# Fourteen tiny loads behind the weight load of the third last group of a batched matmul

## The chip, the core and the metric

The kernel runs on one core of one Trainium2 chip. The metric is the device time in microseconds. Three runs of the kernel before gave 518.32, 518.4 and 518.6 us, median 518.4.

## The reference

```python
b1, b2, m, k, n = 8, 16, 256, 512, 384
x:      (b1, b2, m, k) float32, weight: (b1, b2, k, n) float32
np.matmul(x, weight).astype(np.float32)
```

So there are 128 independent products of a 256x512 matrix with a 512x384 matrix. Inputs are 64 MiB of x and 96 MiB of weights, the output is 48 MiB.

## The kernel before

The 128 products are taken in NG = 32 groups of G = 4. For a group, x is 1024 rows of 2 KB, laid on 128 partitions with 8 rows each (`x_sb`, 2 MB); the weight is 2048 rows of 1.5 KB, laid on 128 partitions with 16 rows each (`w_sb`, 3 MB); the output is 1024 rows (`out_sb`, 1.5 MB). There are two buffers of `x_sb`, two of `w_sb` and four of `out_sb`.

Each engine runs its own written-out program, and semaphores tie them together:

- SP (`on_sync`) issues all transfers, on one DMA queue. `load_x` (L108) first waits until the casts of the group two earlier have freed the buffer; `load_w` (L125) waits likewise for the casts on VectorE and ScalarE (L119, L120); `store` (L138) waits until the output has been copied out. Per group the order is `load_x(n)`, `store(n - 4)`, `load_w(n)`. The first four groups stand ahead of a loop (groups 4 to 27), the last four behind it (L256 to L260). The first four groups and the last two are "short": their weight load goes out in two halves. Group 31 has no store between its loads. After the loads come the stores of groups 27 to 31, the last in four pieces (L262), and a wait for the completion semaphores of all four output buffers (L264).
- VectorE (`on_vector`) casts x to bf16 (L149, four instructions a group) and 11 of the 16 pieces of the weight (L162, or L178 for short groups).
- TensorE (`on_tensor`) transposes x against an identity (L201) and multiplies (L219).
- ScalarE (`on_scalar`) copies the transposes out of PSUM (L188), casts the other 5 pieces of the weight (L162) and copies the products to `out_sb` (L233).

A completed transfer adds 16 to its semaphore. x, weights and output have their own semaphores for each buffer (`x_in`, `w_in` or `h_in`, `o_out`).

The change touches the declarations at the top (behind L98) and the end of `on_sync` (L256 to L264).

Of the kernel before, what the change touches and what calls it, by code (L numbers as in the profile page):

```python
# [12 lines left out]
def kernel(  # L13
# [14 lines left out]
    x_rows = x.rearrange("b1 b2 m k -> (b1 b2 m) k")  # L28
# [3 lines left out]
    fp32 = mybir.dt.float32  # L32
# [13 lines left out]
    NG = B // G  # L46
# [15 lines left out]
    def sbuf(name, shape, dtype, n):  # L62
        return [
            ctx.enter_context(nc.sbuf_tensor(f"{name}{s}", shape, dtype)) for s in range(n)
        ]
# [6 lines left out]
    def sems(name, n):  # L72
        return [tc.alloc_semaphore(f"{name}{s}") for s in range(n)]
# [22 lines left out]
    )  # L96
    x_in, w_in, o_out = sems("x_in", XS), sems("w_in", WS), sems("o_out", OS)
    h_in = sems("h_in", G)  # L98


    BIAS = 8
# [2 lines left out]
    def load_x(e, t, U, s):  # L104
        n = t * U + s
        if not isinstance(n, int) or n >= XS:
            e.wait_ge(x_cast, n * T + (1 - XS) * T)
        e.dma_start(  # L108
            x_sb[s % XS][:],
            x_rows[bass.ds(n * (G * M), G * M)].rearrange("(p r) k -> p r k", r=R),  # L110
        ).then_inc(x_in[s % XS], 16)

    def is_short(n):
        return isinstance(n, int) and (n < LAG or n >= NG - 2)

    def load_w(e, t, U, s):
        n = t * U + s
        if not isinstance(n, int) or n >= WS:
            e.wait_ge(w_vcast, n * CV + (1 - WS) * CV)  # L119
            e.wait_ge(w_acast, n * CA + (1 - WS) * CA)  # L120
        d = SL // SH if is_short(n) else 1
        k = SL * KO // d
        for h in range(d):
            sem = h_in[s % WS * 2 + h] if is_short(n) else w_in[s % WS]
            e.dma_start(  # L125
                w_sb[s % WS][:, h * k : (h + 1) * k, :],
                w_rows[bass.ds(n * (G * K) + h * (G // d * K), G // d * K)].rearrange(
                    "(p k) n -> p k n", k=k
                ),
            ).then_inc(sem, 16)  # L130

    def store(e, t, U, s, pieces=1):
        n = t * U + s
        dram = o_rows[bass.ds(n * (G * M), G * M)].rearrange("(p r) n -> p r n", r=R)
        for q in range(pieces):
            rows = slice(q * R // pieces, (q + 1) * R // pieces)
            e.wait_ge(o_copied, n * T + ((q + 1) * T // pieces + BIAS))
            e.dma_start(out=dram[:, rows], in_=out_sb[s % OS][:, rows]).then_inc(  # L138
                o_out[s % OS], 16
            )  # L140
# [103 lines left out]
    def on_sync(e):  # L244
        U = OS
        for n in range(LAG):
            load_x(e, 0, NG, n)
            load_w(e, 0, NG, n)
        rounds = (NG - 2 - LAG) // U
        with e.Fori(0, rounds) as t:  # L250
            for s in range(U):
                load_x(e, t, U, LAG + s)
                store(e, t, U, s)
                load_w(e, t, U, LAG + s)

        for n in range(LAG + rounds * U, NG):  # L256
            load_x(e, 0, NG, n)
            if n < NG - 1:
                store(e, 0, NG, n - LAG)
            load_w(e, 0, NG, n)  # L260
        for n in range(NG - 1 - LAG, NG):
            store(e, 0, NG, n, T if n == NG - 1 else 1)  # L262
        for s in range(OS):
            e.wait_ge(o_out[s], 16 + 16 * (NG // OS + (T - 1 if s == (NG - 1) % OS else 0)))  # L264

# [75 lines left out]

    on_gpsimd(nc.gpsimd)
    on_sync(nc.sync)
    on_vector(nc.vector)
    on_tensor(nc.tensor)
# [31 lines left out]
```

## Time and profile before

| | |
|---|---|
| median of three runs | 518.4 us (518.32 to 518.6) |
| span of the profiled execution, first to last instruction | 516.8 us |
| time of the profiled execution beyond its span | not given by the page |
| mean granted TensorE clock | 0.780 |
| ScalarE, VectorE, TensorE busy | 410.3, 397.7, 315.2 us |
| x loads | 32 of 2048 KB, median 22.3 us from issue to landing |
| whole weight loads | 26 of 3072 KB, 18.1 us |
| half weight loads | 12 of 1536 KB, 16.6 us |
| whole stores | 31 of 1536 KB, 25.4 us |
| store pieces | 4 of 384 KB, 5.6 us |
| HBM traffic | 167.77 MB read, 50.33 MB written |

The span is cut by the page into 40 equal slices; a digit there is the busy share of an engine, or of the 16 DMA engines together, in tenths. Times within the span count from its first instruction. A load or store of this kernel leaves 16 completion marks, one for each DMA engine; the trace has the time of each, and of every DMA packet.

### The profile page before, as it was taken

How to read it: one execution, taken by the hardware profiler on the slowest of the kernel's cores; microseconds unless marked ns; L12 is line 12 of the kernel's file. 1: busy time of each engine (PE TensorE's matmuls, PEld its weight loads, DVE VectorE, ACT ScalarE, POOL GpSimd, SP SyncE). 2: the span in 40 equal slices, each digit the busy share in tenths (PEclk: the TensorE clock that was granted, in tenths of full speed). 3: DMA queues.
4: the chain of work that ended last, by engine and by line, in shares of the span. 5: the costliest groups of instructions: out<-in, count | busy, mean ns of one | idle time of the engine just before them, and what ended most of it. 6: DMA issues, size and time to landing. Idle time of an engine off the chain costs nothing.

```text
span 516.8 us, 11572 instructions
## 1 busy us (share of the span) xinstructions
PE 315.2 (61%) x4608; PEld 225.4 (44%) x4608; DVE 397.7 (77%) x462; ACT 410.3 (79%) x387; POOL 0.7 (0%) x6
## 2 busy tenths in 40 slices
PE   2277838555676675765475766558656667565681
PEld 2255525444454443454353544435534445344550
DVE  2788757798777897777987778977779777797960
ACT  1365666998797989798979879978989897899561
POOL 0000000000000000000000000000000000000000
PEclk9687786878786778787778868776867786688887
DMA  8999999999999999999999999999999999999995
GB/s 335 426 428 425 435 429 423 431 430 434 429 424 431 432 439 434 424 426 433 434 434 431 422 432 433 435 429 428 425 438 429 440 428 420 433 433 429 424 428 219
DMA packets 15127, 218.19 MB, mean 422 GB/s; under 512 B 1680, under 2 KB 1680, under 8 KB 2192
## 3 DMA queue, kind: packets, MB, share of 16 engines
q1 hardware_dynamic: 15120, 218.11, 99.0%
q8 instruction: 3, 0.05, 0.0%
q14 instruction: 4, 0.03, 0.0%
HBM read 167.77 MB, written 50.33 MB: 422 GB/s over the span
## 4 chain that ended last, share of the span: by engine, by line
DMA 57%; DVE 29%; issue 9%; PE 1%; SPq 1%; DVEq 1%; ACT 0%
DMA w_sb<-in_weight_dram 57%; DVE w_bf L162 20%; DVE x_bf L149 5%; DVE w_bf L178 4%; PE po L219 1%; SPq L125 0%; DVEq L288 0%; SPq L108 0%; DVEq L158 0%; ACT out_sb L233 0%; SPq L120 0%; DVEq L146 0%; DVEq L172 0%; SPq L372 0%; SPq L60 0%
## 5 line engine op out<-in xcount | busy, mean ns | idle before, releaser
L162 DVE CAST w_bf<-w_sb 32x1536 bf16<-32x1536 f32 x286 | 271.9, 951 | 81.6 <-DMA w_sb<-in_weight_dram 73.5
L219 PE MATMUL po<-w_bf,x_t 128*32 128x384 bf16 x4096 | 200.6, 359 | 38.3 <-DVE w_bf L162 21.0
L201 PE MATMUL pt<-identity,x_bf 128*128 128x128 f32 x512 | 115.0, 415 | 152.2 <-DVE x_bf L149 152.2
L162 ACT CAST w_bf<-w_sb 32x1536 bf16<-32x1536 f32 x130 | 190.9, 1468 | 6.0 <-DMA w_sb<-in_weight_dram 2.8
L201 PEld LDWEIGHTS pt<-identity,x_bf 128*128 128x128 f32 x512 | 103.4, 224 | 164.1 <-issue 163.8
L219 PEld LDWEIGHTS po<-w_bf,x_t 128*32 128x32 bf16 x4096 | 122.0, 106 | 115.9 <-issue 40.7
L233 ACT COPY out_sb<-po 128x768 f32<-128x768 f32 x128 | 101.5, 803 | 57.3 <-PE po L219 56.6
L188 ACT COPY x_t<-pt 128x1024 bf16<-128x1024 bf16 x128 | 120.3, 1025 | 22.1 <-PE pt L201 21.5
L149 DVE CAST x_bf<-x_sb 128x1024 bf16<-128x1024 f32 x128 | 80.0, 688 | 12.4 <-DMA x_sb<-in_x_dram 11.5
L178 DVE CAST w_bf<-w_sb 64x1536 bf16<-64x1536 f32 x48 | 45.9, 955 | 8.3 <-DMA w_sb<-in_weight_dram 7.0
L188 ACT ACT_TABLE_LOAD x1 | 1.3, 1283 | 10.8 <-PE pt L201 10.8
masks.py:199 POOL TENSOR_SCALAR_AFFINE_SELECT identity<-identity 128x128 f32<-128x128 f32 x1 | 0.3, 294 | 0.2 <-POOL identity L239 0.2
L239 POOL MEMSET identity<- 128x128 f32 x1 | 0.2, 205 | 0.5 <-SPq L60 0.5
L361 POOL MEMSET const-bfloat16-1.0<- 128x1 bf16 x1 | 0.1, 102 | 0.0
L361 POOL MEMSET const-uint8-127<- 128x1 uint8 x1 | 0.1, 102 | 0.0
L361 POOL MEMSET const-float32-0.0<- 128x1 f32 x1 | 0.1, 99 | 0.2 <-issue 0.2
L361 POOL MEMSET const-float32-1.0<- 128x1 f32 x1 | 0.1, 99 | 0.0
## 6 DMA issues: line engine op xcount, KB each, us to landing
w_sb<-in_weight_dram SPq DMA_DIRECT2D x26, 3072.0 KB, 18.1
x_sb<-in_x_dram SPq DMA_DIRECT2D x32, 2048.0 KB, 22.3
out_dram<-out_sb SPq DMA_DIRECT2D x31, 1536.0 KB, 25.4
w_sb<-in_weight_dram SPq DMA_DIRECT2D x12, 1536.0 KB, 16.6
out_dram<-out_sb SPq DMA_DIRECT2D x4, 384.0 KB, 5.6
```

The costliest lines, as they stand in the source:

```text
L149: e.tensor_copy(out=x_bf[s % BS][:, rows].rearrange("p r (s q c) -> p r s q c", s=S, c=KO), in_=x_sb[s % XS][:, rows].rearrange("p r (q s ...
L162: copy(out=w_bf[(s * G + i) % WBS][h * C : (h + 1) * C], in_=w_sb[s % WS][i * C : (i + 1) * C, h * KO : (h + 1) * KO, :],).then_inc(w_vcas ...
L178: e.tensor_copy(out=w_bf[(n * G + d * SH + a) % WBS][h * p : (h + 1) * p], in_=w_sb[n % WS][a * p : (a + 1) * p, r : r + KO, :],).then_inc ...
L188: e.copy(out=x_t[s % TS][:, 2 * q : 2 * q + 2], in_=pt[(s * T + q) % PT][:].bitcast(bf16),).then_inc(t_copied, 1)
L201: ins = e.transpose(pt[(s * T + q) % PT][:, rr, h, :], words[:, 2 * q + rr, h :: KO // 2], identity[:],)
L219: ins = e.matmul(po[(s * T + q) % PO][mine, rr, :N], x_t[s % TS][:, 2 * q + rr, ko // 2, mine, ko % 2], w_bf[(s * G + i) % WBS][:, ko, :], ...
L233: e.copy(out=out_sb[s % OS][:, 2 * q : 2 * q + 2, :], in_=po[(s * T + q) % PO][:, :, :N],).then_inc(o_copied, 1)
L239: e.memset(identity[:], 0.0).then_inc(id_done, 1)
L361: nc = _bacc.Bacc("TRN2", target_bir_lowering=False, num_devices=1)
```

## The change

Sixteen small buffers of 16 rows of 64 bytes and sixteen semaphores are declared. When the loads of group 29 (NG - 3) have been issued, fourteen loads follow: for k from 2 to 15, k rows of 64 bytes each, from the first 16 columns of the rows 16k and on of x, into the first k partitions of a buffer of their own, each with its own semaphore. They wait for nothing, and nothing of the computation reads these buffers. At the end, SP waits for the fourteen semaphores too.

```diff
     h_in = sems("h_in", G)
+    probe = sbuf("probe", [16, 16], fp32, 16)
+    few_in = sems("few_in", 16)
...
             load_w(e, 0, NG, n)
+            if n == NG - 3:
+                for k in range(2, 16):
+                    e.dma_start(probe[k][:k], x_rows[16 * k : 17 * k, :16]).then_inc(few_in[k], 16)
         for n in range(NG - 1 - LAG, NG):
             store(e, 0, NG, n, T if n == NG - 1 else 1)
+        for k in range(2, 16):
+            e.wait_ge(few_in[k], 16)
         for s in range(OS):
```

In the built program the fourteen loads stand on SP directly behind the weight load of group 29 and ahead of the wait for the x buffer of group 30. No other engine's order is changed.

## Prediction

> **What bounds the kernel now.** I read the page's share by queue first, then its forty slices, then the chain of waits, SP's timeline from 449 us, and last the windows of the final six microseconds.
>
> ```profile
> span 516.8 us, 11572 instructions
> ...
> DMA  8999999999999999999999999999999999999995
> ...
> q1 hardware_dynamic: 15120, 218.11, 99.0%
> ```
>
> SP's one queue keeps the 16 DMA engines busy for 99.0% of the span, from the second slice to the last but one. No compute engine is above 79%. The page's chain names DVE casts and weight loads in turn, but that chain cannot be shortened below the bytes: one group is 2 MB of x, 3 MB of weight and 1.5 MB of output. The windows of one group each (416.7 to 432.6, 449.2 to 465.1 and 465.1 to 481.0) last 15.90 us at 429 to 432 GB/s with a DMA share of 1.00 to 1.01. So DMA bounds the kernel up to its last stores. Now SP near the end:
>
> ```profile
> 432.58 0.34 SPq L125 DMA_DIRECT2D w_sb<-in_weight_dram  x1
> 432.97 0.42 SPq L108 DMA_DIRECT2D x_sb<-in_x_dram  x1
> 433.44 0.43 SPq L138 DMA_DIRECT2D out_dram<-out_sb  x1
> 449.25 0.33 SPq L125 DMA_DIRECT2D w_sb<-in_weight_dram  x1
> 449.62 0.43 SPq L108 DMA_DIRECT2D x_sb<-in_x_dram  x1
> 450.10 0.44 SPq L138 DMA_DIRECT2D out_dram<-out_sb  x1
> 465.13 0.81 SPq L125 DMA_DIRECT2D w_sb<-in_weight_dram  x2
> 465.99 0.44 SPq L108 DMA_DIRECT2D x_sb<-in_x_dram  x1
> 481.03 0.81 SPq L125 DMA_DIRECT2D w_sb<-in_weight_dram  x2
> ```
>
> Columns are start and duration. SP issues for 1.3 us a group and then stands at a weight wait (L120, L125) for some 14 us. Group 29's weights go out at 449.25, and the tiny loads will stand directly behind them. The chain of waits, in order of time, has this load landing 18.36 us later, the last one 11.08:
>
> ```profile
> 449.25 18.36 DMA w_sb<-in_weight_dram
> ...
> 481.03 11.08 DMA w_sb<-in_weight_dram
> ```
>
> The sixteen completion marks of each load in the trace tell more. Those of x(29), issued at 432.97, fall at 452.58 to 456.58; of store(25), issued next, at 456.23 to 460.31; of w(29) at 463.51 to 467.61; of x(30) at 468.40 to 472.46. Thus the queue is served in order, it is over 14 us deep at 449.6, and the slowest DMA engine is 4 us behind the first. That spread is 3.2 us at 416, 3.9 at 437, 4.1 at 476 and 5.4 at 506. It sets the end:
>
> ```profile
> 509.00:510.00 1.00, 0.00 (x0) 0.00 (x0) 0.00 (x0) 0.00 (x0) 0.00 (x0) 1.00 0.92 372
> 510.00:511.00 1.00, 0.00 (x0) 0.00 (x0) 0.00 (x0) 0.00 (x0) 0.00 (x0) 1.00 0.45 181
> 511.00:512.00 1.00, 0.00 (x0) 0.00 (x0) 0.00 (x0) 0.00 (x0) 0.00 (x0) 0.55 0.22 89
> 512.00:513.00 1.00, 0.00 (x0) 0.00 (x0) 0.00 (x0) 0.00 (x0) 0.00 (x0) 0.50 0.06 25
> 513.00:514.00 1.00, 0.00 (x0) 0.00 (x0) 0.00 (x0) 0.00 (x0) 0.00 (x0) 0.50 0.07 28
> 514.00:515.00 1.00, 0.00 (x0) 0.00 (x0) 0.00 (x0) 0.00 (x0) 0.00 (x0) 0.50 0.05 22
> ```
>
> The last two columns are DMA share and GB/s. A share of 0.06 is one engine in sixteen: from 512.1 to 514.9 one laggard works alone. The last store piece lands at 515.31 and SP's final wait (L264) ends at 515.3; 1.5 us of closing instructions follow. The piece was issued at 506.60, while the first engine finished its share only at 510.41. So compute is not late here: the last matmuls could slip some 2.8 us (510.41 less 506.60 less about 1 us, the time from the first issue at 0.96 to the first packet at 1.98) before any engine missed them.
>
> **The change, part by part.**
>
> *SP's issues.* Fourteen issues are put ahead of x(30) at 449.62; they wait for nothing. A tiny issue is not in the trace. The nearest rows are back-to-back issues of 128 rows, 0.43 us plus 0.05 between, 0.48 together; the longest, in the opening microseconds, took 0.66, so 0.71. The lower end is one 0.05 us gap each. That makes 0.7 to 9.9 us; I take 14 x 0.48 = 6.7 us, since the instruction is of the same form. Behind it on SP stand x(30), store(26) and the wait for w(30). x(30) then goes out at 456.3, store(26) at 456.8, and SP is at its weight wait by 457.3, where it stands until 465.13 anyway: w(30) is not moved. In the queue, x(30) is needed when w(29) is done, 463.51 on the first engine; less 1.0 us from issue to first packet, that is 462.5. Cover is 12.9 us, or 0.92 us a load. Cost: **nothing**, and bandwidth is not lost even at 9.9.
>
> *The rows themselves.* 2 + ... + 15 = 119 rows of 64 bytes, 7.6 KB in all, and a completion mark on each engine used. Spread over 430 GB/s, the bytes are 0.02 us. What counts is the row as a packet: a mark of 4 bytes took 0.009 us in the packet records, a 3072-byte row of the last stores 0.121 us. One row and one mark cost an engine between 0.018 and 0.13 us; by size the row is far nearer to the mark, and I take 0.02 with its mark. No engine can have fewer than 0 or more than 14 of either (one row per load), so the laggard pays 0 to 1.8 us; with half of them, 7 x 0.02 = **0.14 us**. The other engines pay too, but have 3 us and more to spare against the laggard.
>
> The Trainium skill ("DMA: Bandwidth & Descriptors", Why a DMA increments its semaphore by 16 and not by 1) says that such a load uses as many engines as divide both row counts, the lowest-numbered ones, and that the issuing sequencer writes the missing part of the 16 itself. By that rule engines 0 and 1 get 14 rows, engine 14 one, engine 15 none, and the sum would be 0 to 0.28 us instead of 0.14; no run here shows it yet.
>
> *The waits at the end.* The built program's order on SP puts fourteen more semaphores into the final wait; two of them stand behind that of the last store. The loads themselves land by about 470 at the latest, so each wait is met. An SP wait of this kind takes 17 to 28 ns, 0.05 to 0.08 us from start to start; the ones ahead run during the last store's flight (506.9 to 515.3). Two are on the path: **+0.1 us**, bounds 0 and 0.4 (should all of them come after).
>
> *Sum.* 516.8 + 0 + 0.14 + 0.1 = 517.0 us of span, bounds 516.8 and 519.0. The page gives no time of the profiled execution beyond its span; the three runs shown (518.32, 518.4, 518.6) have their median 1.6 us above it. I carry that over: **518.6 us**, +0.05%, where 0.2% (1.04 us) is about what a measurement of this kernel can tell from no change. "Same" thus reaches from 517.4 to 519.4.
>
> **Rivals.**
>
> *Each tiny load exposes a latency (slower).* At the start, when the queue was empty, 16 KB packets took 1.04 to 1.94 us instead of the usual 0.61: 0.43 to 1.33 us of exposed start-up. If an engine could not run on past a tiny row before it has come, it would pay this per load: 14 x 0.43 = 6.0 us, at most 14 x 1.33 = 18.6. On the laggard all of it shows; on the second-latest engine (done at 512.1) what exceeds 3.1 us; on the earliest what exceeds 4.9. It decides from 0.22 us a load (3.1/14). Result: 518.4 + 6.0 - 4.9 = 519.5 at the least, 537 at the most; by the second-latest engine at 0.43, 521.3, and 524.4 on the laggard. Against it: over a group the packets of x (8 x 0.612 + 0.009), w (8 x 0.912 + 0.009) and store (8 x 0.46 + 0.009) add up to 15.9 us, exactly the group's length, so marks and the reads behind them hide completely. But those reads are 12 to 24 KB, and 14 tiny ones in a row have no such length to hide in. The skill's same page (Rules for kernel authors) advises coalescing small transfers, as under 64 KB one pays mostly overhead; its fixed cost of about 2.0 us for a DMA (Anatomy of one DMA, told of GpSimd's path) would make 28 us if nothing overlapped. The trace speaks against that: the four 384 KB stores end 1.0 us apart. Chance 0.22.
>
> *The queue runs dry (slower).* If a tiny issue took over 0.92 us, x(30) would come late for the first engine; the laggard, which has w(29) until 467.61, is hit from (466.6 - 449.6)/14 = 1.21 us. At 1.4 us: 14 x 0.19 = 2.7 us lost, 521.1. Twice the longest issue of the trace is needed. Chance 0.05.
>
> *The laggard pays several small things (slower).* The upper bounds of the rows and the waits together, 1.8 + 0.4: 520.6. Chance 0.04.
>
> *The laggard gets rid of something (faster).* Two 8 KB instruction fetches (at 422.41 and 498.88 us in the packet records) stand where its lag jumps, 3.2 to 3.9 and 4.1 to 5.4. SP's program becomes longer by 14 loads and some waits, which can move a fetch in time or to another engine. If both jumps missed the laggard: 518.4 - 0.7 - 1.3 = 516.4. Nothing shows that these are SP's fetches, and one fetch alone stays within 0.2%. Chance 0.12.
>
> That the loads are not made at all is excluded: the built program has all fourteen, directly behind w(29).
>
> **How the numbers follow.** Hidden, 518.6: 0.57. Slower: 0.22 + 0.05 + 0.04 = 0.31. Faster: 0.12. The range goes from 517.3, which leaves out most of the faster case, to 522.0, which takes in the bounds of the sum (520.6) and the lower half of the latency case: some 0.1 is left out on either side. The forecast's own range is 517.9 to 519.4.
>
> **What would show it.** Right: SP issues x(30) near 456, w(30) still at 465.1; x(30) lands within 0.5 us of 468.40 to 472.46; no slice of the DMA row falls between 450 and 480; one engine alone still ends the run. Wrong: packets of 64 bytes that take over 0.2 us or with gaps behind them, a spread of x(30)'s marks grown by 3 us or more, or a DMA share under 0.9 from 463 to 470.

## The result and the profile after

Nine runs of the changed kernel have a median of 519.92 us (519.62 to 520.04), nine of the kernel before 518.56 us (518.29 to 519.11). The ratio is 1.0026, 95% interval [1.0016, 1.0036]: 1.36 us slower, inside the predicted range (517.3 to 522.0) and outside the forecast's own range (517.9 to 519.4). The profiled execution took 519.66 us, its span is 517.9.

The page of the changed kernel (lines are cut out):

```profile
span 517.9 us, 11593 instructions
...
DMA  8999999999999999999999999999999999999994
...
DMA packets 15365, 218.20 MB, mean 421 GB/s; under 512 B 1918, under 2 KB 1918, under 8 KB 2430
...
q1 hardware_dynamic: 15358, 218.12, 98.9%
```

The queue is as full as before. There are 238 packets more: 119 rows and 119 marks, so each row went with a mark of its own, that is each load used as many DMA engines as it has rows. SP's timeline, with start and duration:

```profile
448.98 0.33 SPq L127 DMA_DIRECT2D w_sb<-in_weight_dram  x1
449.35 5.17 SPq L265 DMA_DIRECT2D probe<-in_x_dram  x14
454.56 0.39 SPq L110 DMA_DIRECT2D x_sb<-in_x_dram  x1
455.00 0.43 SPq L140 DMA_DIRECT2D out_dram<-out_sb  x1
464.85 0.80 SPq L127 DMA_DIRECT2D w_sb<-in_weight_dram  x2
465.70 0.44 SPq L110 DMA_DIRECT2D x_sb<-in_x_dram  x1
```

The fourteen issues take 5.2 us, x(30) goes out 4.9 us later than before, and the weight issue of group 30 does not move (464.85; before 465.13). The loss appears later, in the chain of waits, where a weight load stands with its start and its time to landing:

```profile
448.98 18.39 DMA w_sb<-in_weight_dram
...
480.79 12.44 DMA w_sb<-in_weight_dram
```

The load directly ahead of the tiny ones lands as before (18.39 against 18.36 us); the first half of the last one takes 1.36 us longer (12.44 against 11.08). Between them lie the tiny loads. In the windows around their passage the last two columns are DMA share and GB/s; first the kernel after, then the kernel before:

```profile
463.00:465.00 2.00, 0.89 (x5) 0.48 (x3) 1.79 (x2) 1.97 (x3) 0.00 (x0) 0.50 1.08 339
465.00:467.00 2.00, 1.91 (x28) 1.01 (x31) 0.00 (x0) 2.00 (x3) 0.00 (x0) 0.50 1.00 386
```

```profile
463.00:465.00 2.00, 0.83 (x6) 0.64 (x4) 1.94 (x3) 1.98 (x3) 0.00 (x0) 0.92 0.92 393
465.00:467.00 2.00, 1.67 (x44) 1.16 (x48) 0.11 (x1) 2.00 (x3) 0.00 (x0) 1.00 1.02 434
```

The engines move fewer bytes there (339 and 386 GB/s against 393 and 434) at a share of 1.08 and 1.00 against 0.92 and 1.02. A full share is thus no proof of full rate: from 463 to 470 us, 19 packets of 16 KB took 0.71 to 1.79 us instead of the usual 0.61 (before, none took over 0.65), and all of that counts as busy.

The end is as it was, about a microsecond later:

```profile
510.00:511.00 1.00, 0.00 (x0) 0.00 (x0) 0.00 (x0) 0.00 (x0) 0.00 (x0) 0.75 0.68 273
...
513.00:514.00 1.00, 0.00 (x0) 0.00 (x0) 0.00 (x0) 0.00 (x0) 0.00 (x0) 0.50 0.06 25
514.00:515.00 1.00, 0.00 (x0) 0.00 (x0) 0.00 (x0) 0.00 (x0) 0.00 (x0) 0.50 0.07 28
515.00:516.00 1.00, 0.00 (x0) 0.00 (x0) 0.00 (x0) 0.00 (x0) 0.00 (x0) 0.50 0.05 22
```

One engine alone (0.06 of sixteen) ends the run again, now until 515.9 instead of 514.9.

**Which engine pays, and what.** The completion marks name it. The last mark of each tiny load, by its number of rows k, comes at 464.88 (k = 2), 465.05, 465.23, then 467.55 (k = 5), 467.74, 467.93 and so on to 469.47 (k = 15). Up to k = 4 the latest engine is not in the load; from k = 5 it is. So the laggard is the fifth engine in the order in which loads take them, and it carried 11 of the 14 loads. Its marks stand 0.19 us apart, although a row packet takes 0.011 us and a mark 0.009. From its mark of w(29) to that of the last tiny load pass 467.37 to 469.47 = 2.10 us; from there to its mark of x(30) at 473.57 another 4.10. Before, x(30) followed w(29) on it in 4.85 us (467.61 to 472.46). The loss is 2.10 + 4.10 - 4.85 = **1.35 us**, the whole difference of the medians. So 0.75 of the 2.10 is won back. The packet records show how far the reads had run ahead: one engine has eleven tiny rows in a row there, which is the laggard; they start at 466.87 to 467.00, 0.013 us apart, and its first packet of x(30) starts directly behind, at 467.01, before the first of its tiny marks lands. That packet then takes 1.27 us instead of 0.61.

### The profile page after: what moved, and what is told of

The parts are those of the page before. It is cut to its first block, busy times and chain, and to the rows that moved or that the text cites. A ratio compares the mean times of both kernels' runs of the same rounds, so it can differ in the third digit from the quotient of the medians.

```text
span 517.9 us, 11593 instructions
## 1 busy us (share of the span) xinstructions
PE 309.9 (60%) x4608; PEld 223.9 (43%) x4608; DVE 397.7 (77%) x462; ACT 410.0 (79%) x387; POOL 0.7 (0%) x6
## 4 chain that ended last, share of the span: by engine, by line
DMA 57%; DVE 29%; issue 9%; PE 1%; SPq 1%; DVEq 1%; ACT 0%
DMA w_sb<-in_weight_dram 57%; DVE w_bf L164 20%; DVE x_bf L151 5%; DVE w_bf L180 4%; PE po L221 1%; SPq L127 0%; DVEq L295 0%; SPq L110 0%; DVEq L160 0%; ACT out_sb L235 0%; DVEq L148 0%; SPq L122 0%; DVEq L174 0%; SPq L379 0%; SPq L60 0%
## 5 line engine op out<-in xcount | busy, mean ns | idle before, releaser
L221 PE MATMUL po<-w_bf,x_t 128*32 128x384 bf16 x4096 | 196.1, 353 | 39.7 <-DVE w_bf L164 27.5
```

What stands on the lines that cost most here:

```text
L221: ins = e.matmul(po[(s * T + q) % PO][mine, rr, :N], x_t[s % TS][:, 2 * q + rr, ko // 2, mine, ko % 2], w_bf[(s * G + i) % WBS][:, ko, :], ...
```

## The experiments

The theory after this: a tiny load costs each engine that carries it 0.19 us once, not per row, and only the laggard's sum counts, less 0.75 us that is won back once in an unbroken chain. The rivals: SP's issues ahead of x(30); the semaphores and waits at the end; the number of rows.

**Four rows and five rows.** One row more decides whether the laggard takes part.

```diff
-                    e.dma_start(probe[k][:k], x_rows[16 * k : 17 * k, :16]).then_inc(few_in[k], 16)
+                    e.dma_start(probe[k][:4], x_rows[16 * k : 16 * k + 4, :16]).then_inc(few_in[k], 16)
```

> Fourteen loads as in the change, at the same place and with their own semaphores and waits, but each of 4 rows of 64 bytes. Theory (the change costs only what the one late DMA engine pays; by its completion marks that engine is the fifth, it carries a row of the loads with k from 5 to 15 and none of a load with 4 rows): the late engine pays nothing, the others have over 2 us to spare, so the time is that of the kernel before within 0.1% (518.6 us), and the last mark of x(30) stays at about 472.4 us. Rival (SP's issues ahead of x(30), or the fourteen waits at the end, make the loss): still 519.9 us.

> The same fourteen loads with 5 rows each: one row more a load than in the run with 4 rows. Theory of the late fifth engine: it now carries all fourteen loads instead of eleven, so it pays 14/11 of 1.35 us = 1.7 us: 520.3 us, and its marks of the tiny loads are 0.19 us apart. Rival (issues or waits): the same as with 4 rows. Rival (bytes or number of rows in all count: 70 rows here, 119 in the change): 0.8 us, 519.4.

With 4 rows 518.6 us against 518.45, ratio 1.0002 [0.9993, 1.0012]; with 5 rows 520.63, ratio 1.0043 [1.0029, 1.0057]. In the chains of waits the last weight load is that of the kernel before with 4 rows, and 1.9 us longer with 5; first the run with 4 rows, then that with 5:

```profile
481.12 11.08 DMA w_sb<-in_weight_dram
```

```profile
481.23 12.99 DMA w_sb<-in_weight_dram
```

Both issue fourteen loads (5.1 and 5.5 us) and wait for fourteen semaphores. That settles it against issues and waits. The laggard's marks with 5 rows go from 468.00 to 470.49, 0.19 us apart; x(30) on it takes 6.76 us instead of 4.85, a loss of 1.91 (14 x 0.19 - 0.75); the medians differ by 2.2, with an interval of 1.5 to 3.0.

**One load of 14 rows for each engine.**

```diff
+                e.dma_start(
+                    probe[0][:15],
+                    x_rows[: 15 * 14].rearrange("(p r) k -> p r k", r=14)[:, :, :16],
+                ).then_inc(few_in[0], 16)
```

> Instead of the fourteen loads one load into 15 partitions with 14 rows of 64 bytes for each: the late engine gets 14 rows, more than in the change, but one completion mark and SP one issue. Theory that the mark costs, because it waits for its row to come and holds what stands behind it: 0.1 to 0.2 us, 518.7 us. Rival that every tiny row costs by itself (its read is exposed): 14 x 0.12 = 1.7 us or more, 520.3. The issues ahead of x(30) and the waits at the end are gone too; the run with 4 rows tells whether they matter.

518.75 us, ratio 1.0005 [0.9996, 1.0014]. The laggard's mark comes 0.19 us after that of w(29) (467.85 and 467.66): fourteen rows and one mark cost as much as one row and one mark. So the price is paid per load, and rows cost next to nothing. The Trainium skill ("DMA: Bandwidth & Descriptors", Anatomy of one DMA) says, of GpSimd's path, that the semaphore update cannot fire before the last byte is confirmed, and that the update itself is nearly free. These loads are issued by SP; the runs fit both, but prove neither: the mark's packet takes 0.009 us, the spacing is 0.19. The packet records speak against a start-up ahead of each load, since the changed kernel's rows on the laggard start 0.013 us apart and only the landings of their marks are 0.19 apart. What a mark waits for stays open.

**Spread out.** Fourteen loads of 5 rows, one behind each load or store from group 28 on and behind the first three stores at the end.

```diff
             load_x(e, 0, NG, n)
+            tiny(e)
             if n < NG - 1:
                 store(e, 0, NG, n - LAG)
+                tiny(e)
             load_w(e, 0, NG, n)
+            tiny(e)
```

> Fourteen loads of 5 rows with their own semaphores as in the run that took 520.63 us, but one at a time: one behind each load or store that SP issues from group 28 on, and behind the first three stores at the end. Theory (a completion mark waits some 0.17 us for its row, and only a row of such waits without a large load between them can not be hidden by reads that run ahead): 0 to 0.4 us over the kernel before, 518.5 to 518.9. Rival (each load costs its engine 0.156 us wherever it stands): 520.6 again.

518.71 us, ratio 1.0007 [0.9998, 1.0017]: of the 2.2 us that the same loads cost in a row, 0.3 are left, not clear of nothing. The laggard's tiny mark still lands 0.19 us behind that of w(29) (467.51 and 467.70), but x(30) ends on it 4.88 us behind w(29), before 4.85: behind a single large transfer such a pause is made up.

**One semaphore for all, sixteen rows, twice as many.** Loads of 5 rows on one semaphore; loads of 16 rows; 28 loads of 5 rows.

```diff
-        for k in range(2, 16):
-            e.wait_ge(few_in[k], 16)
+        e.wait_ge(few_in[0], 14 * 16)
```

> The fourteen loads of 5 rows behind the loads of group 29, all on one semaphore, so one wait at the end instead of fourteen. Theory that the marks cost by standing in a row on the DMA engine, whichever semaphore they go to: 520.6 us as with fourteen semaphores. Rival (the number of semaphores, or of waits at the end, has a part in it): less, down to 518.5.

> Fourteen loads of 16 rows: every engine gets one row of each, 224 rows instead of 70. Theory (only the late engine's own row and mark count): 520.6 us as with 5 rows. Rival (the cost grows with the engines or rows that take part, or engines that all wait at once lose the bandwidth that the late one had been lent): well above, 522 or more.

> Twenty-eight loads of 5 rows behind the loads of group 29 instead of fourteen. Theory (each load more in the row costs the late engine the same 0.156 us; SP's 28 issues take 9.6 us and stay under the 12.9 us of queued work): 518.4 + 28 x 0.156 = 522.8 us. Rival (a fixed cost for the row as a whole, or a part of the 2.18 us that comes once): nearer to 521.5.

One semaphore: 520.4 us, 1.0037 [1.0024, 1.0051]. Sixteen rows: 520.46, 1.0038 [1.0024, 1.0051]. Neither differs from the run with 5 rows on fourteen semaphores beyond the intervals, though sixteen rows is three times the rows. Twenty-eight loads: 524.1 us, 1.0108 [1.0093, 1.0124], more than the 522.8 expected. Two things were missing there. The 0.75 us is won back once, not per load: 28 x 0.19 - 0.75 = 4.6 us instead of 4.4. And the laggard's lag of 8.4 us now passes the slack of the computation: the weights of group 31 land so late that the store of group 30 is issued at 504.41 instead of 499.76, and the other engines run dry, as the window around that issue shows (share 0.74, 313 GB/s):

```profile
504.00:506.00 2.00, 1.02 (x28) 0.79 (x32) 0.74 (x1) 0.38 (x1) 0.00 (x0) 1.00 0.74 313
```

One more thing shows in SP's timeline of this run:

```profile
449.22 10.09 SPq L265 DMA_DIRECT2D probe<-in_x_dram  x28
459.35 0.36 SPq L110 DMA_DIRECT2D x_sb<-in_x_dram  x1
459.75 2.58 SPq L140 DMA_DIRECT2D out_dram<-out_sb  x1
```

A single store issue took 2.58 us, otherwise 0.33 to 0.44. It stands right behind the 28 loads and x(30); the 28 loads themselves still went out at 0.36 us each. That the number of outstanding transfers makes it is not shown.

**Early, and in the middle.** The loads of the change behind the first four groups; loads of 5 rows between groups 15 and 16, with SP's loop cut in two, and the cut loop alone.

```diff
         for n in range(LAG):
             load_x(e, 0, NG, n)
             load_w(e, 0, NG, n)
+        for k in range(2, 16):
+            e.dma_start(probe[k][:k], x_rows[16 * k : 17 * k, :16]).then_inc(few_in[k], 16)
```

> The fourteen loads of the change, 2 to 15 rows, moved from behind the loads of group 29 to behind those of group 3, at about 35 us. Theory (whatever the late engine loses is never won back, as its queue is never empty until the end, wherever it is lost): about 519.9 us again. Rival (only the end of the kernel is sensitive, or the loss is caught up in the 480 us that follow): 518.6 us. A time well above 519.9 would say that SP's issues delay the early loads, where the queue is less deep.

> The fourteen loads of 5 rows between groups 15 and 16, about 230 us, for which SP's loop is cut into two loops of three turns each. Theory (what the late engine loses is not won back while its queue stays full): the run with the cut loops alone plus 2.0 to 2.2 us, about 520.5. Rival (lag is won back over the 230 us that follow): within 0.5 us of the run with the cut loops.

> The kernel before with SP's loop cut into two loops of three turns, no tiny loads: what the run with the loads in the middle is to be compared with. Expected within 0.5 us of the kernel before, since SP waits some 14 us in each group; it differs from 518.4 only if the longer program moves an instruction fetch on or off the late engine.

In the middle 521.0 us, ratio 1.0046 [1.0032, 1.0060], against 518.36 with the cut loop alone, 0.9999 [0.9990, 1.0008]: 2.6 us, where 2.0 to 2.2 were expected. The spread of the marks grows from 2.7 to 4.6 us as the tiny loads pass, by 247 us, and is 5.9 at 463; it stands 1.96 us above that of the cut loop at 247 and still 1.8 at 463. What the laggard loses in the middle is thus hardly won back in 216 us. The rest of the 2.6 comes at the end: SP issues the weights of group 31 at 482.68 instead of 480.90, and from 488 to 492 us 358 GB/s are moved instead of 424. Early it is 519.19, 1.0020 [1.0009, 1.0030]: 0.74 us by the medians, half of the expected loss. There an instruction fetch had moved from 422 to 89 us, which the next run tries.

**The instruction fetch.** Fourteen increments of an unused semaphore ahead of SP's loop, no loads.

```diff
+        for k in range(14):
+            e.sem_inc(pad[0], 1)
         rounds = (NG - 2 - LAG) // U
```

> The kernel before with fourteen semaphore increments (on a semaphore that nobody waits for) on SP ahead of its loop and no tiny load: SP's program becomes as much longer as by fourteen loads put there. In the run with the loads at group 3 the instruction fetch that stood at 422 us had moved to 89 us and the late engine's lag no longer jumped by 0.75 us there, and that run cost 0.74 us instead of 1.36. Theory that moving the fetch takes it off the late engine: 0.75 us faster than before, 517.7. Rival that the fetch only moves in time and still falls on the same engine: 518.45, no difference, and then the early loads cost less for another reason.

518.17 us against 518.38, ratio 0.9994 [0.9985, 1.0003]. The fetch moves to 87.9 us as foreseen, the jump of the lag at 422 (3.2 to 3.9) is gone, and the lag at 475 us is 3.7 instead of 4.15; but the median falls by 0.2 us alone, with an interval from 0.8 faster to 0.2 slower. So the fetch is SP's. By the medians, moving it explains the early loads' smaller cost only in part: 0.74 + 0.21 = 0.95 of 1.35. But the interval of the early run reaches from 0.5 to 1.6 us, so it is not shown that a rest is missing.

**Taking work from the laggard.** The stores of groups 28 and 29 as one of 112 partitions and four of 4.

```diff
+        for a, z in ((0, 112), (112, 116), (116, 120), (120, 124), (124, 128)):
+            e.dma_start(out=dram[a:z], in_=out_sb[n % OS][a:z]).then_inc(o_out[n % OS], 16)
```

> The kernel before, no tiny loads; the stores of groups 28 and 29 go out as one of 112 partitions (7 for each engine instead of 8) and four of 4 partitions, which by the run with 4 rows use the first four engines alone. Theory that the fifth engine's lag sets the end: it is relieved of 2 x 0.46 us, the first four get 2 x 1.38 us more and end at about the same time: 0.9 us faster, 517.5 us. Rival (something else sets the end, or the split costs more than it saves): 518.45 or slower.

522.0 us, 1.0073 [1.0060, 1.0087]: 3.6 us slower instead of 0.9 faster. The windows of this run, then those of the kernel before:

```profile
490.00:500.00 10.00, 8.74 (x144) 6.43 (x143) 8.88 (x11) 6.96 (x8) 0.00 (x0) 0.84 1.03 403
500.00:510.00 10.00, 5.57 (x128) 3.70 (x128) 0.23 (x1) 3.10 (x4) 0.00 (x0) 1.00 0.94 312
```

```profile
490.00:500.00 10.00, 8.88 (x144) 5.97 (x143) 8.98 (x11) 6.97 (x8) 0.00 (x0) 0.83 1.01 428
500.00:510.00 10.00, 5.39 (x128) 3.77 (x128) 0.10 (x1) 3.20 (x4) 0.00 (x0) 1.00 0.99 412
```

At a nearly full share only 312 instead of 412 GB/s are moved: a packet of 12 KB that starts between 490 and 510 us takes 0.539 us on the mean instead of 0.463, the longest 2.5. The last group's copies then came late, since they wait for the store of group 27:

```profile
503.00 1.50 ACT L233 COPY out_sb<-po 128x768 f32<-128x768 f32 x2 [3.41 <-DMA out_dram<-out_sb]
```

SP was slow there too: its issues of the last three store pieces took 2.32, 2.11 and 1.65 us, before 0.33, so the last went out at 509.03 although its copy had ended at 507.57. That packets and issues are slow with the split is shown, why is not: the rows per engine, the small stores and the shifted assignment of partitions to engines changed together. Nothing here beats the kernel before beyond its interval.

## Why the prediction was right and wrong

- **SP's issues cost nothing: right.** They took 5.2 us (6.7 forecast), x(30) went out at 454.6, the weight issue did not move, and with 4 rows the same issues cost nothing that can be measured.
- **The waits at the end cost little: right.** The closing instructions behind the last mark take 1.6 us, before 1.5; one wait instead of fourteen saves 0.2 us, inside the intervals.
- **"The rows themselves": this term was mis-sized, and it is the whole loss.** It priced a row and a mark by their packets, 0.02 us, for 7 loads: 0.14 us. Measured are 11 loads of 0.19 us less 0.75 won back, 1.35 us. Packet durations do not hold the time between the landings of two marks. The bound of 1.8 us did hold the value, but by luck: it priced a load at 0.13 us at most, and the loss stayed below it because three of the fourteen loads pass the laggard by and 0.75 us is won back. With all fourteen on it (5 rows) the loss was 1.91.
- **The argument that the group's packets add up to 15.9 us, so marks hide, was right for large loads alone.** The spread-out run confirms it there (0.3 us for fourteen). In a row with nothing large between them marks do not hide, as the rival had said.
- **The rival of the exposed latency had half the mechanism and not the size.** A cost per load it is; but it let the engine stand still at each row, and the packet records show rows and reads going on while the marks land 0.19 us apart. Its 0.43 us a load was taken from the start of the run; 0.19 was measured, below its deciding point of 0.22. That point held for the second-latest engine; it did not cover what decided, that the laggard itself carries 11 of the loads.
- **The other rivals did not come.** An issue took 0.37 us a load, under the 0.92 at which the queue would run dry. The two instruction fetches stand as before (421.52 and 499.08 us), and the lag still jumps there.
- **The end set by one laggard: right**, and it is the reason why 5 rows cost and 4 do not. That the time was forecast within 0.2% fell with the row term: it is 0.26%. The time lies in the wide range because that took in the rivals and the upper bounds.
- **The signs.** Of those named for "right", one failed: the last mark of x(30) came at 473.57, 1.11 us late and not within 0.5. None of those named for "wrong" came: a row's packet took 0.011 us, the spread of x(30)'s marks grew from 4.06 to 5.11 us, and the DMA share was 0.98 to 1.08 from 463 to 471. They were set for a far greater loss.
- **The Trainium skill's rule on the number of engines** ("DMA: Bandwidth & Descriptors", Why a DMA increments its semaphore by 16 and not by 1) agrees with the trace: 119 marks, each load on as many engines as rows, always the same ones first. With it, the laggard is the fifth of them.

## What to carry to other kernels

Where one DMA queue bounds a kernel, look at the sixteen completion marks of a load, not at the last one: the engine that is late sets the end, and only what that engine carries costs time as long as the others stay ahead of it (here the next latest was 1.8 us ahead at w(29) and 3.1 at the end, before the change). Price a tiny load by the spacing of marks in a row (0.19 us here) and not by its packets (0.02 us); put tiny loads singly behind large ones, or merge them into one, and most of their cost is gone. What the late engine lost in the middle of the run was still missing at the end.

## What the runs showed of the hardware that was not expected

- The sixteen engines move equal bytes and still drift apart, not evenly: in the kernel before the spread of the marks is 2.3 us from 203 to 258 us, grows to 2.5 at 305 and 3.16 at 416 (0.006 us per microsecond), and by another 1.2 us between 492 and 506. The cause was not found.
- A store issue on SP took 2.58 us with 28 tiny loads, w(29) and x(30) ahead of it, and three took 1.65 to 2.32 us behind the split stores; with fourteen tiny loads no issue took over 0.81.
- A tiny issue took 0.25 to 0.39 us in the changed kernel, 0.26 to 0.48 with 5 rows and 0.42 to 0.49 with 16, hardly less than one of 128 partitions (0.33 to 0.44). The single load of 14 rows for each of 15 partitions took 1.09.
- Stores split over 112 and 4 partitions moved 312 GB/s where stores over 128 partitions moved 412.
